# Hybrid encoder layer on one core: ten pairs of projection tiles by seven products each, attention two heads at a time beside a two-part output projection

## The chip, the cores and the metric

The kernel runs on one core of a Trainium2 chip. The time is device microseconds of one execution, from three runs. Everything is computed in float32; a float32 product is made exact from three products of shortened operands (below).

## The reference

768 tokens (512 of a prompt, 256 of a sample) of width 2048 pass one layer. What is computed, shortened:

```
h = rms_norm(x)                      # scale by (mean of x*x + eps) ** -0.5, times a gain per feature
p = h @ w_in                         # 2048 -> 8192 features, and 32 more for decay and beta
A: 8 heads x 128: softmax(q k^T / sqrt(128) + ALiBi and window bias) v, times SiLU(gate_A)
B: 8 heads x 128: short conv on q, k, v, gated delta rule in both directions,
   RMSNorm per head, times SiLU(gate_B)
y = rms_norm(x + concat(A, B) @ w_out)
```

## The kernel before

Features lie on the 128 partitions and tokens on the free axis, so the input projection makes 64 feature tiles of 128 x 768 tokens: tiles 0 to 7 q, 8 to 15 k, 16 to 23 v and 24 to 31 gate of the attention heads, 32 to 55 q, k and v and 56 to 63 gate of the delta heads. A tile runs over 16 K tiles of 128. Weights and inputs are split exactly into a high and a low part (`hip` and `lop` of the weights, `xh` and `xl` of the inputs), and `kstep` adds three products per K tile, high x high, high x low and low x high, each as one matmul of 512 columns (prompt, bank `mm_0`) and one of 256 (sample, bank `mm_1`): 96 matmuls of 384 columns in the mean for a tile, 6144 for all. The weights come as blocks of 128x512 (256 KB) and are split in pieces of 256 columns: ScalarE copies the high part, VectorE or, for every other piece, GpSimd subtracts it for the low part (`w_split`).

x is split as it arrives, before its norm is known: x times the gain is `xh_x`, `xl_x`, and the factor of each token (`rB`, the same in all partitions) is multiplied in after the products, by VectorE on the way out of PSUM (`normed` and `conv_post`). The sum of squares behind `rB` is added up in `x_squares`, mostly on GpSimd (`xacc`).

The order of the tiles stands in `jobs`: first the delta heads, q, k, v and the gate of the head before, then the attention heads one by one, q, k, v and a gate, with four attention gates after the last head, and at the end the output projection. While a tile is projected, `Driver` sets steps of other work between the groups of matmuls (`slot`): convolutions, the delta rule of one head, or one attention head (`attend`, tag `attend`, one at a time). `Driver` keeps a rough clock of each engine and takes, of the steps whose inputs are due, the one with the best priority; all this is settled when the program is built. Each engine then runs its own instructions in the order in which they were written, so an instruction that waits holds up all that stand behind it on the same engine.

In an attention head, S is scores (three products per tile of 128 queries), `s` the softmax on VectorE and ScalarE, T its transposes, PT the transposed weights split in two (ScalarE copies, VectorE subtracts), and o the product with v.

The output projection takes the 16 K tiles of the mixed features, delta heads first, in four quarters of 512 output columns and six tiles of 128 tokens: 48 matmuls of 128x512 for each group (`mmo`), 1152 in all, with nothing but the splitting of its own weights (`oh`, `ol`) and the end of each group (`o_post`: add the residual, square, gain) beside it. Three quarters go out to `yD` and come back for the last.

Instructions are recorded by helpers, so in the profile all matmuls have line L272, transposes L277, other operations L192 and loads or stores L234; in the changed kernel these are L280, L285, L200 and L242. Tiles are told apart by name.

Of the kernel before, what the change touches and what calls it, by code (L numbers as in the profile page):

```python
# [6 lines left out]
F32 = mybir.dt.float32  # L7
# [16 lines left out]
# columns of the constant array  # L24
# [3 lines left out]
def constants():  # L28
# [4 lines left out]
        # sums over the tokens up to i (from i on), counted from the middle of the tile  # L33
# [14 lines left out]
HOP = 0.12       # us from an instruction's end to one on another engine that waits for it  # L48
EARLY = 1.0      # us by which steps without products are emitted ahead of their inputs
SIDE_MAX = 3     # side steps between two groups of products  # L50
DEEP = 2.5       # us of work queued on VectorE beyond which bulk steps hold back
LOOK, AHEAD = 3, 4     # half stages by which weights are split, loaded ahead
DEC_P = 5        # priority of the decays
SUB_P, SUB_N, SUB_E = -6, 2, 1.0    # the inversions: priority, columns at a time, head start
LATE = 4         # attention gates that are projected after the last head


class Driver:
    """Orders the work as it is emitted. It keeps a rough clock of every engine; the projections' products run on,
    and the steps of the side tasks go between them once their inputs are due."""  # L60
# [32 lines left out]
    def ran(self, eng, cost, outs, ins, extra=0.0):  # L93
        """an instruction was emitted: its time by the rough clocks"""
# [10 lines left out]
    def placed(self, tag, ap, bufs):  # L105
        """a new tile in one of a tag's places: it waits for the place's last reader"""
# [16 lines left out]
    def free(self, tag, n=1):  # L123
        """can n more of the tag's places be had? (a place is given back once its last reader is emitted)"""
# [11 lines left out]
    def until(self, cond):  # L136
        """emit side steps until the condition holds"""
# [1270 lines left out]
```

## Time and profile before

| | |
|---|---|
| runs | 1663.59, 1667.91 and 1667.31 us, median 1667.31 |
| profiled execution | span 1662.0 us from its first to its last instruction, 1.6 us under the shortest run and 5.3 under the median; what lies around the span isn't shown apart |
| instructions | 27562, of them 10283 matmuls (transposes among them) |
| TensorE busy | 1615.9 us (97%) |
| VectorE busy | 841.0 us (51%) |
| ScalarE busy | 736.3 us (44%) |
| GpSimd busy | 416.3 us (25%) |
| traffic with memory | 125.65 MB read, 22.86 MB written, 89 GB/s over the span |

Busy time counts running instructions only. Matmuls overlap, so the mean duration of one (some 0.4 us for 512 columns) is longer than the distance between the starts of two; where a text speaks of the pace of matmuls it means that distance. In rows, PE is TensorE, DVE VectorE, ACT ScalarE, POOL GpSimd and SP the queue of loads and stores. "Idle before, releaser" and the waits name what ended an engine's idle time.

### The profile page before, as it was taken

The numbers are of one execution on the slowest core, as the hardware profiler recorded it, in microseconds if no ns is written. First come the engines' busy times: TensorE is split into PE (matmuls) and PEld (weight loads), VectorE is DVE, ScalarE is ACT, GpSimd is POOL, SyncE is SP. The second block draws the span as 40 slices with busy tenths as digits, with TensorE's granted clock in tenths as the row PEclk, the third lists the DMA queues.
The fourth block names the chain that finished last, engine by engine and source line by source line (L and its number), as shares of the span: only waits on it lengthen the run. The fifth ranks groups of instructions, "written<-read, shape, count | busy, mean of one in ns | idle before, by whom it ended". The sixth has DMA issues, their size and how long they took to land.

```text
span 1662.0 us, 27562 instructions
## 1 busy us (share of the span) xinstructions
PE 1615.9 (97%) x10283; PEld 1392.2 (84%) x10283; DVE 841.0 (51%) x1956; ACT 736.3 (44%) x1861; POOL 416.3 (25%) x430
## 2 busy tenths in 40 slices
PE   5999999999999999999999999999999999999997
PEld 4788788888888888898888888888888888888885
DVE  6758674857677767675343342425334336313132
ACT  5575546564765566553433232424333335202121
POOL 4443413232424242332121222222121210111100
PEclk9999999999999999999999999999999999999999
DMA  5232312232323232313212222221221256534365
GB/s 190 61 89 72 97 47 79 64 87 59 83 62 87 65 80 65 87 47 84 67 49 79 65 61 69 61 75 55 78 75 57 72 188 224 158 91 118 90 200 180
DMA packets 107783, 150.32 MB, mean 90 GB/s; under 512 B 40864, under 2 KB 48128, under 8 KB 107648
## 3 DMA queue, kind: packets, MB, share of 16 engines
q1 hardware_dynamic: 105632, 143.83, 29.8%
q10 hardware_dynamic: 2016, 4.72, 0.7%
q8 instruction: 81, 1.33, 0.3%
q14 instruction: 54, 0.44, 0.1%
HBM read 125.65 MB, written 22.86 MB: 89 GB/s over the span
## 4 chain that ended last, share of the span: by engine, by line
PE 78%; DVE 9%; DMA 5%; ACT 4%; issue 3%; SPq 1%; POOL 0%; DVEq 0%; POOLq 0%; ACTq 0%
PE mm L272 55%; PE mmo L272 11%; PE c L272 5%; DVE lop L192 2%; PE o L272 2%; PE S L272 2%; DMA res<-in_x 1%; PE m L272 1%; DVE tmp L192 1%; PE kk L272 1%; PE T L277 1%; DMA xst<-in_xT 1%; DVE cacc L192 1%; DMA st<-in_wt 1%; DVE PB L192 1%
## 5 line engine op out<-in xcount | busy, mean ns | idle before, releaser
L272 PE MATMUL mm<-xl_x,hip 128*128 128x512 f32 (+1 forms) x2048 | 541.4, 345 | 7.6 <-DVE xl_x L192 7.6
L272 PE MATMUL mm<-xh_x,hip 128*128 128x512 f32 (+1 forms) x2048 | 538.0, 344 | 8.8 <-ACT hip L192 7.7
L272 PE MATMUL mm<-xh_x,lop 128*128 128x512 f32 (+1 forms) x2048 | 539.5, 345 | 0.0
L192 POOL TENSOR_TENSOR lop<-st,hip 128x256 fp32r<-128x256 f32 x252 | 205.8, 817 | 817.7 <-ACT hip L192 744.9
L272 PEld LDWEIGHTS mm<-xh_x,hip 128*128 128x128 f32 x2048 | 315.1, 189 | 52.2 <-ACT hip L192 8.1
L272 PEld LDWEIGHTS mm<-xl_x,hip 128*128 128x128 f32 x2048 | 315.9, 190 | 49.3 <-DVE xl_x L192 9.2
L272 PEld LDWEIGHTS mm<-xh_x,lop 128*128 128x128 f32 x2048 | 316.6, 190 | 41.4
L192 ACT CAST hip<-st 128x256 fp32r<-128x256 f32 x512 | 202.0, 402 | 328.0 <-PE mm L272 254.3
L192 DVE TENSOR_TENSOR lop<-st,hip 128x256 fp32r<-128x256 f32 x260 | 146.9, 566 | 323.7 <-ACT hip L192 313.4
L272 PE MATMUL mmo<-oh,xh_m 128*128 128x512 f32 x384 | 151.7, 395 | 0.4 <-DVE yt_a L192 0.4
L272 PE MATMUL mmo<-ol,xh_m 128*128 128x512 f32 x384 | 151.7, 395 | 0.0
L272 PE MATMUL mmo<-oh,xl_m 128*128 128x512 f32 x384 | 151.6, 395 | 0.0
L192 DVE TENSOR_TENSOR PB<-PB,tmp 88x30 f32<-88x30 f32 (+14 forms) x240 | 91.4, 381 | 8.2
L192 DVE TENSOR_TENSOR tmp<-PB 88x30 f32<-88x30 f32 (+14 forms) x240 | 92.2, 384 | 6.1 <-ACT PB L192 1.5
L272 PEld LDWEIGHTS mmo<-oh,xh_m 128*128 128x128 f32 x384 | 72.4, 189 | 17.6 <-DVE yt_a L192 0.9
L272 PEld LDWEIGHTS mmo<-ol,xh_m 128*128 128x128 f32 x384 | 72.4, 189 | 16.8
L272 PEld LDWEIGHTS mmo<-oh,xl_m 128*128 128x128 f32 x384 | 72.5, 189 | 16.7
L192 DVE TENSOR_TENSOR yt<-mmo,res 128x512 f32<-128x512 f32 x18 | 12.4, 690 | 126.9 <-PE mmo L272 92.6
L192 POOL TENSOR_TENSOR cacc<-cacc,ctmp 128x772 f32<-128x772 f32 x32 | 58.9, 1841 | 58.3 <-ACT ctmp L192 54.2
L192 ACT ACTIVATE s<-s,m 128x512 f32<-128x512 f32 (+1 forms) x48 | 31.3, 653 | 92.8 <-DVE m L192 92.8
L192 POOL TENSOR_TENSOR yt<-yt,fg 128x512 f32<-128x512 f32 x18 | 23.2, 1291 | 190.5 <-ACT res L192 190.5
L192 ACT ACTIVATE res<-yt 128x512 f32<-128x512 f32 x18 | 11.4, 632 | 132.7 <-DVE yt L192 132.7
(198 smaller groups left out, 1880.7 us busy)
## 6 DMA issues: line engine op xcount, KB each, us to landing
st<-in_wt SPq DMA_DIRECT2D x256, 256.0 KB
ost<-in_wo SPq DMA_DIRECT2D x32, 512.0 KB
dec<-gcD SPq DMA_DIRECT2D x24, 256.0 KB
xl_m<-mixD SPq DMA_DIRECT2D x16, 384.0 KB
res<-in_x SPq DMA_DIRECT2D x24, 256.0 KB
out_y<-row SPq DMA_DIRECT2D x12, 512.0 KB
xst<-in_xT SPq DMA_DIRECT2D x15, 384.0 KB
yD<-yt SPq DMA_DIRECT2D x18, 256.0 KB
```

Source lines behind the costliest of these rows:

```text
L192: r = f(*a, **k)
L272: r = PE.matmul(out, lhsT, rhs, start=start, stop=stop)
L277: r = PE.transpose(out, in_, ident)
```

## The change

**Input projection.** Ten pairs of feature tiles (v of all attention heads, their gates, and four delta gates) are computed by Strassen's scheme in Winograd's form. For a pair, rows are two feature tiles, columns the two halves of 384 tokens, and K goes in two phases of 2 x 4 K tiles; in each phase seven products of 4 K tiles take the place of eight (`PRODUCTS`, `pair_products`), every one with three matmuls of 384 columns per K tile: 84 a phase, 168 a pair, where two tiles had 192. The combinations of the weights (S1 to S4) are made by VectorE as the weights come, those of the inputs (T1 to T4) once for all pairs (`block_sums`), and the products are combined out of three PSUM banks X, Y and Z by VectorE (`evacuate`). Weights are split 512 wide, in a ring of six tiles.

**Order.** Four delta gates are projected first, two tiles at a time on x as it arrives. Then x is normalised in place (`norm`, new `xh_n` and `xl_n`), q and k of the first attention head follow tile by tile behind it, then the ten pairs, then the other 38 tiles singly. The multiplications with `rB` behind the projections fall away but for those four gates. q, k, v and gates of the attention heads wait in memory (`qD`, `kD`, `vD`, `agD`, `gD`) till they are needed. The additions of squares go from GpSimd to VectorE.

**Attention and output projection.** Two heads run at a time on two sets of buffers (`SETS`), from the time that the 24 convolutions are done, on into the output projection. This has two parts: part 0 the eight K tiles of the delta heads, for all 24 groups, with the attention beside it; part 1 the eight of the attention heads, to which part 0's result comes back from `yD`. The products with v are taken for two query tiles at a time, 256 columns wide.

```diff
+ORDER, FIRST_ORDER = (1, 6, 5, 2, 7, 3, 4), (1, 2, 5, 6, 3, 7, 4)
+PRODUCTS = {1: ("A11", "X", "B11"), 2: ("A12", "X", "B21"), 3: ("S4", "Z", "B22"), 4: ("A22", "Y", "T4"),
+            5: ("S1", "Z", "T1"), 6: ("S2", "Y", "T2"), 7: ("S3", "Y", "T3")}
...
-                        (V if k >= NK - 2 else G).tensor_tensor(out=xacc, in0=xacc, in1=s, op=ALU.add)
+                        V.tensor_tensor(out=xacc, in0=xacc, in1=t, op=ALU.add)
...
+            def plan_pair(pi, ph, order):
+                f0, f1 = pairs[pi]
+                c0, c1 = 2 * ph, 2 * ph + 1
+                names = dict(A11=(f0, c0), A21=(f1, c0), A22=(f1, c1), A12=(f0, c1))
...
+                            V.tensor_tensor(out=s["S1"], in0=a("A21"), in1=a("A22"), op=ALU.add)
+                            V.tensor_tensor(out=s["S2"], in0=s["S1"], in1=a("A11"), op=ALU.subtract)
+                            V.tensor_tensor(out=a("A21"), in0=a("A11"), in1=a("A21"), op=ALU.subtract)
+                            s["S3"] = a("A21")
...
+                        if name == "S4":
+                            s["S4"] = a("A12")
+                            V.tensor_tensor(out=s["S4"], in0=s["S4"], in1=s["S2"], op=ALU.subtract)
+                        src = s[name] if name in s else a(name)
+                        r = w_split(src, f"p{m}")
...
+            def inputs(ph, name, i):
+                lo, hi = slice(0, HALF), slice(HALF, T)
+                a, b = 8 * ph + i, 8 * ph + 4 + i
+                if name in ("B11", "B21", "B22", "T2"):
+                    k, c = {"B11": (a, lo), "B21": (b, lo), "B22": (b, hi), "T2": (a, hi)}[name]
+                    return xh[k][:, c], xl[k][:, c]
+                t = tset[ph, name, i]
+                return t[:, lo], t[:, hi]
...
+                for n, pr in enumerate(order):
+                    _, b, name = PRODUCTS[pr]
+                    drv.until(lambda: there(ph, name))
+                    new = b not in x["banks"]
+                    if new:
+                        drv.until(lambda: free("mm"))
+                        take("mm")
+                        x["banks"][b] = bank(f"{b}{pi}_{ph}")
+                    else:
+                        drv.until(lambda: all(q in x["ev"] for q in order[:n] if PRODUCTS[q][1] == b))
+                    u, (hi, lo) = piece()
+                    for i in range(4):
+                        v = inputs(ph, name, i)
+                        c = slice(i * P, i * P + P)
+                        for m, (w, j) in enumerate(((hi, 0), (hi, 1), (lo, 0))):
+                            mm(x["banks"][b][:, :HALF], w[:, c], v[j], start=(new and i == 0 and m == 0), stop=(i == 3 and m == 2),
+                               more=True)
+                            if i < 3 or m < 2:
+                                drv.slot()
+                    done_with(u)
+                    drv.end = drv.t + HOP
+                    spawn(evacuate(x, pr), -20)
...
+                need = {1: (), 2: (1,), 3: (5, 6), 4: (5, 6, 7), 5: (1,), 6: (1,), 7: (5, 6)}[pr]
...
+                if pr == 1:
+                    A.copy(s1, X[:, :HALF])
+                elif pr == 6:
+                    V.tensor_tensor(out=u2, in0=Y[:, :HALF], in1=s1, op=ALU.add)
+                    add(u2, 1)
+                elif pr == 5:
+                    V.tensor_tensor(out=t5, in0=Z_[:, :HALF], in1=s1, op=ALU.add)
+                    add(t5, 3)
+                else:
+                    q = {2: 0, 3: 1, 7: 3, 4: 2}[pr]
...
+                    if pr == 2 and not ph:
+                        A.copy(d, X[:, :HALF])
+                    else:
+                        V.tensor_tensor(out=d, in0={2: X, 3: Z_, 7: Y, 4: Y}[pr][:, :HALF], in1={2: d, 3: u2, 7: t5, 4: s1}[pr],
+                                        op=ALU.add)
...
+            def norm():
+                for k in range(NK + 1):
+                    if k < NK:
+                        yield from wait(lambda: reached["raw"] > k)
+                        xn = xstage[k]
+                        V.scalar_tensor_tensor(out=xn, in0=xn, scalar=g_in[:, k:k + 1], in1=rB, op0=ALU.mult, op1=ALU.mult)
+                        xtiles(k, "n")
+                        A.copy(xh[k], xn)
+                    if k:
+                        p = k - 1
+                        V.tensor_tensor(out=xl[p], in0=xstage[p], in1=xh[p].bitcast(F32), op=ALU.subtract)
+                        normal.add(p)
...
+                yield from diff("T1", xa[:, hi], xa[:, lo])
+                yield from high("T1")
+                yield from diff("T2", xb[:, hi], t["T1"])
+                yield from high("T2")
+                low("T1")
+                yield AHEAD
+                yield from diff("T4", xb[:, lo], t["T2"])
+                low("T2")
+                yield from diff("T3", xb[:, hi], xa[:, hi])
+                give(f"t{a}", f"t{a + 4}")
+                yield from high("T4")
+                yield from high("T3")
+                low("T4")
+                low("T3")
+                yield AHEAD
...
-                        V.tensor_tensor(out=cin[:, o:o + width[h]], in0=ps[h][:, :width[h]], in1=rB[:, parts[h]], op=ALU.mult)
+                        A.copy(Z["cin"][:, o:o + width[h]], ps[h][:, :width[h]])
...
+            SETS = (dict(vT="cin", V=("vtok", "vtok"), tab="XT", g="cacc"), dict(vT="ctmp", V=("oacc", "DN"), tab="PB", g="PBT"))
...
+            pairs = ([(16 + j, 17 + j) for j in range(0, NH, 2)] + [(24 + j, 25 + j) for j in range(0, NH, 2)]
+                     + [(56 + j, 57 + j) for j in (4, 6)])
...
+            chain_o = [(part, n, j) for part in (0, 1) for n in range(NQ) for j in range(NH)]
...
+                        ps = bank(f"o{part}{n}_{t}")
+                        o_fetch(part, n, t)
+                        for j in range(NH):
+                            ostep(ps, part, t, j)
+                            between(j)
+                            if t == NT - 1 and j and (part, n) != (1, NQ - 1):
+                                o_split()
+                            drv.slot()
```

On VectorE, the turn from the first to the second phase of the second pair (`lop69` is the low part of the first weights of phase 1, `out1_1` a quarter of the pair's result, mmY and mmZ the banks):

```order
L200 TENSOR_TENSOR lop67_1834<-st35_1716,hip67_1833 128x512
L200 TENSOR_TENSOR sum2_92<-mmZ1_0_1812,sum0_90 128x384
L200 TENSOR_TENSOR lop68_1851<-st34_1676,hip68_1850 128x512
L200 TENSOR_TENSOR lop69_1873<-st36_1718,hip69_1872 128x512
L200 TENSOR_TENSOR out1_1_1877<-mmY1_0_1793,sum2_92 128x384
L200 TENSOR_TENSOR S1_1_1_1890<-st37_1759,st38_1817 128x512
L200 TENSOR_TENSOR S2_1_1_1891<-S1_1_1_1890,st36_1718 128x512
L200 TENSOR_TENSOR st37_1759<-st36_1718,st37_1759 128x512
L200 TENSOR_TENSOR lop70_1896<-S2_1_1_1891,hip70_1895 128x512
```

Nothing of this stood in the kernel before, where VectorE had one subtraction per piece of weights. Product 4 writes bank Y after product 7 has been taken out of it by `out1_1`, which stands behind `lop69`.

On VectorE, the end of the normalisation and the first of eight blocks of input combinations (`xl_n` the low part of normalised x, T1 to T4 the combinations, f as they are and s split; `raw` weights of the gates 58 and 59):

```order
L200 SCALAR_TENSOR_TENSOR xst15_155<-xst15_155,g_in_93,rB_98 128x768
L200 TENSOR_TENSOR xl_n14_1187<-xst14_153,xh_n14_1186 128x768
L200 TENSOR_TENSOR raw43_1205<-st21_999,raw43_1205 128x256
L200 TENSOR_TENSOR raw44_1210<-st22_1031,raw44_1210 128x256
L200 TENSOR_TENSOR xl_n15_1196<-xst15_155,xh_n15_1195 128x768
L200 TENSOR_TENSOR T1f0_1228<-xst0_112 128x384
L200 TENSOR_TENSOR T2f0_1232<-xst4_127,T1f0_1228 128x384
L200 TENSOR_TENSOR T1s0_1230<-T1f0_1228,T1s0_1230 128x384
L200 TENSOR_TENSOR T4f0_1246<-xst4_127,T2f0_1232 128x384
L200 TENSOR_TENSOR xl_n0_714<-T2f0_1232,xh_n0_713 128x384
L200 TENSOR_TENSOR T3f0_1249<-xst4_127,xst0_112 128x384
L200 TENSOR_TENSOR T4s0_1251<-T4f0_1246,T4s0_1251 128x384
```

These are new too: 16 times the two of the normalisation, eight times eight of the combinations.

On TensorE, one attention head before, between matmuls of a projected tile (S4_2: scores of head 4, query tile 2; T4_0_0: transposes of its tile 0):

```order
L277 MATMUL T4_0_0_12559<-ident_404,s4_0_12487 128x128 x4
L272 MATMUL mm5_0_12397<-xh_x13_376,hip414_12472 128x512
L272 MATMUL mm5_1_12398<-xh_x13_376,hip414_12472 128x256
L272 MATMUL mm5_0_12397<-xl_x13_377,hip414_12472 128x512
L272 MATMUL mm5_1_12398<-xl_x13_377,hip414_12472 128x256
L272 MATMUL mm5_0_12397<-xh_x13_376,lop414_12474 128x512
L272 MATMUL mm5_1_12398<-xh_x13_376,lop414_12474 128x256
L272 MATMUL mm5_0_12397<-xh_x14_396,hip415_12502 128x512
L272 MATMUL mm5_1_12398<-xh_x14_396,hip415_12502 128x256
L272 MATMUL mm5_0_12397<-xl_x14_397,hip415_12502 128x512
L272 MATMUL mm5_1_12398<-xl_x14_397,hip415_12502 128x256
L272 MATMUL S4_2_12582<-khi4_12125,qhi4_11899 128x512
```

and in the change, between groups of part 0 of the output projection, heads 2 and 3:

```order
L285 MATMUL T2_4_0_13924<-ident_157,s2_4_13808 128x128 x2
L280 MATMUL S3_2_13929<-khi3_13648,qhi3_13636 128x512
L280 MATMUL S3_2_13929<-qklo3_13567,qhi3_13636 128x512
L280 MATMUL S3_2_13929<-khi3_13648,qklo3_13567 128x512
L280 MATMUL mmo0_2_13706<-oh6_13901,xh_m6_13574 128x512
L280 MATMUL mmo0_2_13706<-ol6_13902,xh_m6_13574 128x512
L280 MATMUL mmo0_2_13706<-oh6_13901,xl_m6_13575 128x512
L285 MATMUL T2_4_1_13947<-ident_157,s2_5_13911 128x128 x2
L280 MATMUL mmo0_0_13704<-oh7_13941,xh_m7_13583 128x512
L280 MATMUL mmo0_0_13704<-ol7_13942,xh_m7_13583 128x512
L280 MATMUL mmo0_0_13704<-oh7_13941,xl_m7_13584 128x512
L280 MATMUL o2_4_1_13958<-PT2_13474,V02_13363 128x256 x4
```

Steps of attention that had ten and more matmuls of a projection between them now stand three output matmuls apart, and belong to two heads.

## Rows read from the trace of the kernel before

**Rows 1.** The page: span, busy time of each engine, chain that ended last.
```profile
span 1662.0 us, 27562 instructions
PE 1615.9 (97%) x10283; PEld 1392.2 (84%) x10283; DVE 841.0 (51%) x1956; ACT 736.3 (44%) x1861; POOL 416.3 (25%) x430
PE 78%; DVE 9%; DMA 5%; ACT 4%; issue 3%; SPq 1%; POOL 0%; DVEq 0%; POOLq 0%; ACTq 0%
```

**Rows 2.** Windows: length, busy us (instructions) by engine, TensorE's granted clock, DMA.
```profile
0.00:40.00 40.00, 23.36 (x102) 17.52 (x102) 26.68 (x24) 21.80 (x33) 19.27 (x13) 0.96 0.58 197
40.00:80.00 40.00, 37.42 (x203) 30.64 (x204) 32.35 (x51) 18.77 (x34) 18.78 (x20) 0.96 0.22 62
...
520.00:560.00 40.00, 36.93 (x368) 31.55 (x367) 22.73 (x56) 27.86 (x73) 17.12 (x18) 1.00 0.35 89
...
1400.00:1440.00 40.00, 40.00 (x174) 32.46 (x173) 5.77 (x9) 4.29 (x11) 5.12 (x4) 1.00 0.39 119
```

**Rows 3.** Waits of TensorE over the span: us in total, times, longest.
```profile
PE mm L272 <- ACT hip L192: 7.7, 2, 7.3
PE kk L272 <- DVE in L192: 7.7, 3, 4.0
PE mm L272 <- DVE xl_x L192: 7.6, 5, 3.1
PE ab L272 <- DVE hab L192: 4.2, 1, 4.2
```

**Rows 4.** The chain in order of time: start, length, what; a stretch of matmuls alone.
```profile
1011.88 36.76 PE mm L272 x212
```

**Rows 5.** Timeline of TensorE: start, duration, instruction; matmuls of 256 columns.
```profile
1156.07 0.28 PE L272 MATMUL S<-khi,qhi 128*128 128x256 f32 x1
...
1156.31 0.28 PE L272 MATMUL S<-khi,qklo 128*128 128x256 f32 x1
```

**Rows 6.** Windows of the start, columns as in rows 2.
```profile
20.00:56.00 36.00, 28.37 (x138) 21.52 (x137) 32.85 (x22) 16.74 (x25) 27.80 (x19) 0.91 0.40 134
32.00:34.00 2.00, 2.00 (x7) 1.45 (x7) 2.00 (x3) 0.35 (x1) 1.50 (x1) 0.50 0.28 70
```

**Rows 7.** Timeline of the start, VectorE and GpSimd.
```profile
9.87 1.02 DVE L192 SCALAR_TENSOR_TENSOR xl_x<-xst,g_in,xh_x 128x768 fp32r<-128x768 f32 x1 [1.65 <-ACT xh_x L192]
...
21.84 6.93 POOL L192 TENSOR_TENSOR xacc<-xacc,xst 128x768 f32<-128x768 f32 x3
...
24.49 2.58 DVE L192 SCALAR_TENSOR_TENSOR xl_x<-xst,g_in,xh_x 128x768 fp32r<-128x768 f32 x1
```

**Rows 8.** Groups of instructions by shape: busy us, mean ns, idle before.
```profile
L192 DVE TENSOR_TENSOR ol<-ost,oh 128x512 fp32r<-128x512 f32 x64 | 42.6, 716 | 17.4 <-ACT oh L192 17.2
...
L192 DVE TENSOR_TENSOR PTl<-T,PTh 128x384 fp32r<-128x384 f32 x32 | 17.7, 554 | 10.5 <-ACT PTh L192 10.5
...
L192 DVE TENSOR_TENSOR xl_m<-xl_m,xh_m 128x768 fp32r<-128x768 f32 x16 | 14.9, 974 | 3.1 <-ACT xh_m L192 3.0
```

**Rows 9.** Groups of ScalarE: the high part of the output weights.
```profile
L192 ACT CAST oh<-ost 128x512 fp32r<-128x512 f32 x64 | 36.2, 617 | 18.4 <-DMA ost<-in_wo 13.5 <-DVE yt_a L192 2.4 <-PE mmo L272 2.2
```

**Rows 10.** Timeline of one attention head.
```profile
1135.15 0.39 PE L272 MATMUL S<-khi,qklo 128*128 128x512 f32 x1
...
1137.50 0.60 PE L277 MATMUL T<-ident,s 128*128 128x128 f32 x4
1137.55 0.49 DVE L192 TENSOR_SCALAR s<-s,m 128x512 f32<-128x512 f32 x1
...
1138.65 0.56 DVE L192 TENSOR_TENSOR PTl<-T,PTh 128x384 fp32r<-128x384 f32 x1 [0.62 <-ACT PTh L192]
...
1139.84 0.43 DVE L192 TENSOR_TENSOR lop<-st,hip 128x256 fp32r<-128x256 f32 x1
```

**Rows 11.** Timeline of the end.
```profile
1650.76 0.39 PE L272 MATMUL mmo<-oh,xl_m 128*128 128x512 f32 x1
1652.50 0.69 DVE L192 TENSOR_TENSOR row<-mmo,res 128x512 f32<-128x512 f32 x1 [6.55 <-DMA res<-in_x]
```

More of the change, by code (lines that the diff above doesn't have):

```diff
@@ new lines, in quarter, with over, prepare @@
+            def quarter(f, c):
+                return wt[f][:, c * 512:(c + 1) * 512]
+            def over(n):
+                dead.add(n)
+                stages.pop(n)
+            def prepare(upto):
+                while cur["made"] <= min(upto, len(plan) - 1):
+                    m = cur["made"]
+                    size, last, make = plan[m]
+                    feed()
+                    if last >= cur["load"] or live and cur["w"] + size - 6 > min(live.values()):
+                        assert m > cur["used"]
+                        break
+                    live[m] = cur["w"]
+                    made[m] = make(m)
+                    cur["w"] += size
+                    cur["made"] += 1
+                feed()
@@ new lines, in attend, with product @@
+                give(S["vT"])
+                yield from get("intra")
+                both = st("intra", (2, 4, 256), f"PT{h}", F32R)
+                qT, kT = (qkv.pop((h, w)) for w in "qk")
+                qkv.pop((h, "lo"))
+                def product(ps, ls, rs):
+                    for c, (l, r) in enumerate(((0, 0), (0, 1), (1, 0))):
+                        m = len(rs[0])
+                        for i in range(m):
+                            mm(ps, ls[l][i], rs[r][i], start=(c == 0 and i == 0), stop=(c == 2 and i == m - 1))
@@ L1082, in attend @@
+                yield lambda: drv.ready(tab) and drv.ready(g)
+                prev = None
+                for t0, t1 in tiles6:
+                    for qi in range(t1 - t0):
+                        s = yield from scores(t0, t1, qi)
                         if prev is not None:
@@ new lines, in leave, with ostep @@
+            def leave(k):
+                left.add(k)
+            for n, (f, post) in enumerate(single):
+                last = n == len(single) - 1
+                if last:
+                    spawn(m_first(), -3)
+                    spawn(w_first(), -2)
+                project(f, post, leave if last else None)
+            def ostep(ps, part, t, j):
+                hi, lo = wset[j]
+                ts = slice(t * P, (t + 1) * P)
+                m = mset[part][j]
+                mm(ps, m[0][:, ts], hi, start=(j == 0), stop=False)
+                mm(ps, m[0][:, ts], lo, start=False, stop=False)
+                mm(ps, m[1][:, ts], hi, start=False, stop=(j == NH - 1))
@@ L1307, in o_post @@
-                if n < NQ - 1:
+                A.activation(ps, yt, AF.Square, accum_out=late["sums"][:, t, n:n + 1])
+                (V if row else G).tensor_tensor(out=yt, in0=yt, in1=gains[n], op=ALU.mult)
+                if not row:
                     return
-                r = op.tile([P, 2], F32, tag="r", name=f"r{t}", bufs=2)
-                V.tensor_reduce(out=r[:, 0:1], in_=sums[:, t], axis=AX.X, op=ALU.add)
+                r = small([2], "r", f"r{t}")
+                V.tensor_reduce(out=r[:, 0:1], in_=late["sums"][:, t], axis=AX.X, op=ALU.add)
@@ L1371, in layout @@
+            while pend or done:
+                between(1)
+                between(3)
+            op_cm.__exit__(None, None, None)
 def layout(i):
```

956 lines of the change are left out of this document (555 added, 401 removed).

## The prediction

> **What bounds the kernel now.** I read the page first, then windows of 40 us, the waits of TensorE, and single stretches. The reader is to see that TensorE is the bound nearly everywhere: it is busy for 1615.9 of 1662.0 us, and the chain that ended last is TensorE for 78% [rows 1]. The other 46.1 us are not spread evenly. By 80 us it has stood idle for 16.6 + 2.6 = 19.2 us [rows 2], made up of three waits: 7.3 for the first weights, 7.6 for low parts of x from VectorE, 4.2 for the split of the small weights [rows 3]. After the last matmul (1650.76) come 11 us of output [rows 11]. The remaining 16 us lie mostly among the delta heads, as in 520 to 560 us, where 3.1 us are lost [rows 2], half of it in waits for one product's input on VectorE, 7.7 us in three [rows 3]. In the output projection nothing is lost: 174 matmuls of 512 columns in 40.00 us, 0.230 us each [rows 2]. So removed matmuls count in full, and new work on VectorE counts where TensorE has to wait for it.
>
> **1. Fewer matmuls.** Twenty tiles need 20 x 84 = 1680 matmuls of 384 columns in place of 1920 of 512 and 256. In the stream of projections 212 matmuls, 384 columns in the mean, take 36.76 us, 0.1734 each [rows 4]. 240 x 0.1734 = **-41.6**. No matmul of 384 columns stands in the trace; 512 columns scaled give 0.230 x 0.75 = 0.1725 [rows 2], 256 columns, 0.24 us for two, give 0.12 x 1.5 = 0.18 [rows 5]. If the 1680 cost that instead of 0.1734 the term runs from -43 to -30; I take the mean that the stream shows, since both widths are in it. The Trainium skill, "TensorE: Matmul & The Clock Gate", section Back-to-back issue gap, has N/2.4 + 2.5 ns for a lone matmul, 162.5 ns at 384 columns; 240 of those would be -39.0, an estimate from that page. The row decides, as the page itself restricts its formula, and 512 columns here take 230 ns against its 216.
>
> **2. The start.** The additions of squares leave GpSimd, where three ran from 21.84 to 28.77 us; beside them a split of x on VectorE took 2.58 us, alone 1.02 [rows 7]. Over 20 to 56 us VectorE was busy for 32.85 of 36 us and TensorE idle for 7.6 [rows 6]. Now VectorE adds them itself: 15 more operations of 768 at about 0.97 [rows 8], 15 us, against 16 x 1.5 us saved on the splits, and it is less full. Two tiles are projected on each arriving K tile, so TensorE has twice as much to do per arrival. I take away the 7.6 of low parts and 1.7 of the 4.2 for the small weights, and add 1.6 for the matmul of the norm, which now sits inside the stream: -7.7, taken as **-7**. Bounds: 0, if VectorE is as late as now, and -12, both waits gone.
>
> **3. VectorE until the first pair is done.** This is the price in front. From the norm on VectorE must do 16 x (1.02 + 0.97) = 31.8 us of normalisation [rows 7, 8], 64 combinations of 384 at 0.554 = 35.5 [rows 8], 32 pieces of weights of 256 at 0.43 = 13.8 [rows 10], and the first pair, 22 operations of 512 at 0.7 plus 13 of 384 at 0.554 = 22.6; with some 2 for the gating's small operations, 106 us. TensorE has for this 4 tiles of 96 x 0.1734 = 66.6 and one pair of 168 x 0.1734 = 29.1, 96 us. The difference stays: **+10**. Low end 0, if the pair can start on its first combinations while the last are made; high end 30, if ScalarE's copy stands between each two of a chain of combinations.
>
> **4. Waits inside a pair.** In the steady state VectorE needs 22.6 us of the 29.1 of a pair, so throughput holds. But product 4 needs bank Y, which product 7 leaves only through `out1_1`, and this stands on VectorE behind the next phase's first `lop`. That `lop` needs a place in the ring, free at the end of product 7. From there: ScalarE's copy of 512 0.617 [rows 9], `lop` 0.716, `out1_1` 0.554 [rows 8], and some 0.4 for three hand-overs make 2.3 us; product 3 between covers 12 x 0.1734 = 2.1. Product 4 waits 0.2, in second phases, where sums stand in front as well, up to 0.9. 20 phases x 0.4 = **+8**, bounds 0 and 18.
>
> **5. Delta heads.** Multiplications with the norm leave VectorE for copies on ScalarE, and GpSimd splits half as many weights. Of the 13 us lost there I give back **-4**; bounds -13 and, as ScalarE takes the copies over, +5.
>
> **6. Attention beside the output projection.** The steps of two heads now stand about three output matmuls apart. From the end of S (about 1135.5) to normalised weights (1138.04) passed 2.5 us, from the start of T (1137.50) to the low part of its split (1139.21) 1.7 [rows 10]. With another head's work between, some 9 us of TensorE's work lie from S to T and 2.1 from T to o, so nothing waits as long as VectorE isn't behind. It is at three turns of quarters, where the splits of new weights, following their predecessor's last products, hold up softmax: **+4**, bounds 0 and 20. Products with v in two halves of 256 cost the same per column [rows 5].
>
> **7. Turn to the second part.** Mixed features of the last heads go out and come back, covered by three groups of 24 x 0.230 = 5.5 us each [rows 2]: **+2**, bounds 0 and 12, where the last store lands late.
>
> **8. Tail.** The last addition waited 1.3 us for its loaded operand [rows 11]; it is now asked for a whole group earlier: **-1**.
>
> Sum: -41.6 - 7 + 10 + 8 - 4 + 4 + 2 - 1 = -29.6. From the span of 1662.0 this gives 1632.4; the median lies 5.3 above the profiled span, so the forecast is **1638**. A change within 0.3% (5 us) can't be told from none.
>
> **The rivals.** *A, the new waits don't come.* Terms 3 and 4 go to 0, since VectorE may work ahead by the buffers there are: -47.6, 1620. For it speaks that VectorE is busy for only 51% [rows 1]; against it, that terms 3 and 4 are chains, not averages. Chance 0.20.
>
> *B, the gain is eaten.* Terms 3 and 4 at their upper ends, 30 and 18: +0.4, 1668. For it speak rows 7, where VectorE was late by 2.5 times its lone duration; against it, that GpSimd, which did that, has nothing in this stretch. Chance 0.07.
>
> *C, the clock.* After the waits of the start TensorE ran at a granted 0.50, its 1.2 GHz, from 32 to 34 us, and 0.91 in the mean over 36 us [rows 6]. If the waits of terms 3 and 4 do the same over the 96 us in front of the first pair, 9% of it, 9 us, are added: 1647. The rule behind it is in the Trainium skill, "TensorE: Matmul & The Clock Gate", Part 1: pauses throttle the array, activity releases it. By that rule the pauses of the wall would cost twice; the trace agrees only for the start. Chance 0.13.
>
> *D, slower: VectorE becomes the bound through all ten pairs.* The point from which it decides: two tiles took 2 x 96 x 0.1734 = 33.3 us, and VectorE's 22.6 us per pair reach that at 1.47 times their lone durations. At 1.8 times a pair takes 40.7, 10 x (40.7 - 29.1) = +116 in place of term 4, together 1738. For it speaks the factor 2.5 in rows 7; against it, that no GpSimd work stands beside the pairs. The Trainium skill, "SBUF — State Buffer", section Who interferes with whom, names an exclusive port between VectorE with two inputs in SBUF and a reading GpSimd; rows 7 agree, and by it this rival fails. Chance 0.06.
>
> **How the numbers follow.** The forecast itself, 1626 to 1650 by one or two terms off, has 0.54. Faster by over 0.3% (under 1662) are it, A, C and a little of B: 0.87. Same are most of B: 0.05; slower D and the rest of B: 0.08. The range leaves out D, most of B, and A where other terms fall low as well: 1608 to 1662.
>
> **What would show it.** In the profile after: 10139 matmuls (240 fewer, 96 more from halves); pairs of 29 to 30 us each; waits of TensorE for `out1` of 0.2 to 0.9 us in pairs, 20 of them; VectorE without a pause from the norm to the first pair, TensorE waiting there for `xl_n` or T1 to T4; a split of x of 1.0 us at the start. The prediction is wrong if a matmul of 384 columns shows another pace than 0.173, if TensorE's first 150 us lose less than 12 us in all or over 45, or if attention costs the output projection more than 20 us.

## The result: slower by 3%, and the profile after

The change takes 1715.16 us (median of four runs, 1714.38 to 1716.2) against 1666.16 us of the kernel before on the same chip: a ratio of 1.0297, 95% interval 1.0283 to 1.0312. The forecast was 1638, and faster. The profiled execution of the change has a span of 1712.7 us, where the forecast had 1632.4.

The page of the change, to be held against [rows 1]:

```profile
span 1712.7 us, 27316 instructions
PE 1605.5 (94%) x10139; PEld 1409.9 (82%) x10139; DVE 1045.0 (61%) x2199; ACT 790.7 (46%) x1784; POOL 259.4 (15%) x225
...
PE 59%; DVE 15%; DMA 9%; ACT 7%; issue 6%; POOL 3%; SPq 2%; DVEq 0%; ACTq 0%; POOLq 0%
```

The 10139 matmuls are the count forecast. But TensorE's share of the chain went from 78% to 59%, and two sums are off. Its idle time is 1712.7 - 1605.5 = 107.2 us; before it was 46.1 [rows 1]. And its busy time should be 1615.9 - 41.6 = 1574.3 us; it is 31 us more.

TensorE's waits of the change (us in total, times, longest), to be held against [rows 3]:

```profile
PE tro L285 <- DVE gate L200: 18.1, 3, 6.0
PE m L280 <- DMA DN<-DD: 17.8, 14, 3.8
PE mmr L280 <- ACT xh_x L200: 10.3, 1, 10.3
PE mmX L280 <- ACT sum L200: 9.1, 1, 9.1
PE trv L285 <- ACT vT L200: 8.7, 4, 6.3
PE mm L280 <- POOL lop L200: 6.8, 6, 1.8
PE mmo L280 <- ACT oh L200: 4.1, 4, 1.6
PE mmo L280 <- DVE ol L200: 3.1, 8, 1.1
PE mmZ L280 <- DVE sum L200: 3.0, 1, 3.0
PE mmY L280 <- DVE out L200: 1.8, 2, 1.2
```

The two largest and the fifth are new, and belong to the delta heads: tro (transposes of a head's output), m (products of the inversion, whose blocks DN come by a detour through memory) and trv (transposes of v). From 440 to 1340 us, the stretch of the delta heads, all waits add up to 55.2 us; in the kernel before, from 60 to 820, to 12.8.

Windows of the change, columns as in [rows 2]; the stretch with the wall (the waits in the first pair), a stretch of pairs, one delta head, the end:

```profile
120.00:160.00 40.00, 27.62 (x134) 25.12 (x133) 36.85 (x73) 20.96 (x43) 0.00 (x0) 0.81 0.19 63
...
200.00:240.00 40.00, 40.00 (x231) 39.60 (x230) 29.79 (x52) 12.94 (x22) 0.00 (x0) 1.00 0.31 93
...
920.00:960.00 40.00, 33.97 (x332) 28.95 (x331) 20.44 (x45) 11.79 (x24) 6.06 (x6) 0.91 0.32 93
...
1680.00:1720.00 40.00, 15.90 (x69) 12.55 (x67) 9.43 (x20) 7.50 (x12) 2.17 (x4) 0.83 0.65 230
```

The pairs are without a gap: 231 matmuls in 40 us, 0.173 each. The head at 920 us loses 6 us to one wait, and its mean clock is 0.91. Where that comes from is seen in three short windows behind the wait:

```profile
921.00:927.00 6.00, 0.32 (x2) 0.00 (x0) 5.54 (x15) 0.31 (x1) 0.00 (x0) 0.93 0.37 136
927.00:929.00 2.00, 1.64 (x6) 1.45 (x7) 1.90 (x6) 0.00 (x0) 0.00 (x0) 0.50 0.00 0
929.00:931.00 2.00, 2.00 (x9) 1.81 (x8) 1.90 (x7) 0.00 (x0) 0.00 (x0) 0.50 0.07 25
```

After 6 us without work TensorE runs at 0.50, 1.2 GHz, and is busy all the time with little more than half the work: two matmuls of 512 and 256 columns start every 0.64 us there (at 928.5), every 0.35 before the wait (at 912). That is the second sum: busy time grows with the waits. The Trainium skill, "TensorE: Matmul & The Clock Gate", Part 1, has the two levels and a throttle that activity releases; the trace agrees.

What kept VectorE, in the timeline of the same head (start, duration, instruction):

```profile
912.00 1.86 POOL L200 TENSOR_TENSOR cacc<-cacc,ctmp 128x772 f32<-128x772 f32 x1 [5.18 <-ACT ctmp L200]
912.14 1.99 DVE L200 TENSOR_TENSOR PB<-PB,tmp 88x238 f32<-88x238 f32 x1
...
913.81 1.44 POOL L200 TENSOR_TENSOR lop<-st,hip 128x512 fp32r<-128x512 f32 x1
...
914.16 1.35 DVE L200 TENSOR_TENSOR tmp<-PB 88x240 f32<-88x240 f32 x1
...
916.28 2.00 POOL L200 TENSOR_TENSOR cacc<-cacc,ctmp 128x772 f32<-128x772 f32 x1
...
916.60 1.95 DVE L200 TENSOR_TENSOR PB<-PB,tmp 88x240 f32<-88x240 f32 x1
...
922.74 0.39 DVE L200 TENSOR_TENSOR tmp<-PB 88x220 f32<-88x220 f32 x1
...
926.56 0.74 DVE L200 SCALAR_TENSOR_TENSOR gate<-tro,dng,gate 128x512 f32<-128x512 f32 x1
...
927.36 0.69 PE L285 MATMUL tro<-ident,oa 128*128 128x128 f32 x2 [6.03 <-DVE gate L200]
```

An operation on PB or tmp of this width takes 0.4 us, but 1.4 to 2.0 where an addition (`cacc`) or a split (`lop`) of GpSimd runs. An inversion is a chain of 60 operations on PB and tmp. The three shown and one of 1.14 us at 919.41 lose 4.8 us together; VectorE has fallen behind, and `gate`, for which TensorE waits 6.03 us, stands in its queue behind them. During the wait itself VectorE runs at full pace. The groups say the same. In the kernel before (mean ns of one after the comma):

```profile
L192 DVE TENSOR_TENSOR lop<-st,hip 128x256 fp32r<-128x256 f32 x260 | 146.9, 566 | 323.7 <-ACT hip L192 313.4 <-PE mm L272 6.9 <-PE tro L277 2.5
...
L192 DVE TENSOR_TENSOR PB<-PB,tmp 88x30 f32<-88x30 f32 (+14 forms) x240 | 91.4, 381 | 8.2
L192 DVE TENSOR_TENSOR tmp<-PB 88x30 f32<-88x30 f32 (+14 forms) x240 | 92.2, 384 | 6.1 <-ACT PB L192 1.5
```

and in the change:

```profile
L200 DVE TENSOR_TENSOR lop<-st,hip 128x512 fp32r<-128x512 f32 x176 | 124.8, 709 | 177.1 <-ACT hip L200 175.2 <-DMA st<-in_wt 1.6
L200 DVE TENSOR_TENSOR PB<-PB,tmp 88x30 f32<-88x30 f32 (+14 forms) x240 | 114.7, 478 | 8.2
...
L200 DVE TENSOR_TENSOR tmp<-PB 88x30 f32<-88x30 f32 (+14 forms) x240 | 102.0, 425 | 22.3 <-ACT PB L200 15.8
```

PB and tmp together take 217 us in place of 184. VectorE's own splits, on the other hand, are hardly stretched any more: 0.709 against 0.69 where GpSimd does none of this work (run e8_conv, below), where those of 256 took 0.566 against 0.43 [rows 10].

Is GpSimd busier beside the delta heads than before? Its two large jobs there, in the kernel before from 60 to 820 us:

```profile
L192 POOL TENSOR_TENSOR lop<-st,hip 128x256 fp32r<-128x256 f32 x137 | 113.1, 827 | 395.2 <-ACT hip L192 331.5 <-PE mm L272 48.2 <-PE c L272 7.4
L192 POOL TENSOR_TENSOR cacc<-cacc,ctmp 128x772 f32<-128x772 f32 x32 | 58.9, 1841 | 58.3 <-ACT ctmp L192 54.2 <-PE mm L272 3.4
```

and in the change from 440 to 1340 us:

```profile
L200 POOL TENSOR_TENSOR lop<-st,hip 128x512 fp32r<-128x512 f32 x75 | 105.3, 1405 | 854.2 <-ACT hip L200 815.8 <-DVE s L200 14.3 <-PE mm L280 11.4
L200 POOL TENSOR_TENSOR cacc<-cacc,ctmp 128x772 f32<-128x772 f32 x32 | 60.5, 1892 | 51.9 <-ACT ctmp L200 51.9
```

It is not: 172 us before, 166 in the change. What differs is what they fall on. Each operation on PB and tmp was held against the same shape in run e8_conv, where neither job runs on GpSimd. By the timelines those that are longer by over 0.1 us lose 58 us in the change, 34 of it beside additions and 22 beside splits; in the kernel before they lose 27, 5 of it beside additions and 19 beside splits.

### The profile page after: what moved, and what is told of

It is laid out like the page before. It is cut to its first block, busy times and chain, and to the rows that moved or that the text cites. A ratio compares the mean times of both kernels' runs of the same rounds, so it can differ in the third digit from the quotient of the medians.

```text
span 1712.7 us, 27316 instructions
## 1 busy us (share of the span) xinstructions
PE 1605.5 (94%) x10139; PEld 1409.9 (82%) x10139; DVE 1045.0 (61%) x2199; ACT 790.7 (46%) x1784; POOL 259.4 (15%) x225
## 4 chain that ended last, share of the span: by engine, by line
PE 59%; DVE 15%; DMA 9%; ACT 7%; issue 6%; POOL 3%; SPq 2%; DVEq 0%; ACTq 0%; POOLq 0%
PE mm L280 21%; PE mmo L280 10%; PE mmY L280 7%; PE mmX L280 5%; PE mmZ L280 4%; PE c L280 4%; DVE tmp L200 4%; DVE PB L200 3%; DMA out_y<-row 2%; SPq L242 2%; PE o L280 1%; PE S L280 1%; PE m L280 1%; PE kk L280 1%; DVE cacc L200 1%
## 5 line engine op out<-in xcount | busy, mean ns | idle before, releaser
L280 PE MATMUL mm<-xh_n,lop 128*128 128x512 f32 x1216 | 326.6, 350 | 8.1 <-POOL lop L200 6.8
L280 PE MATMUL mm<-xl_n,hip 128*128 128x512 f32 x1216 | 327.0, 350 | 0.0
L280 PE MATMUL mm<-xh_n,hip 128*128 128x512 f32 x1216 | 324.5, 348 | 1.2 <-ACT hip L200 1.2
L200 ACT CAST hip<-st 128x512 fp32r<-128x512 f32 x252 | 154.1, 617 | 229.1 <-PE mm L280 88.4
L200 POOL TENSOR_TENSOR lop<-st,hip 128x512 fp32r<-128x512 f32 x76 | 106.6, 1404 | 867.8 <-ACT hip L200 829.5
L200 DVE TENSOR_TENSOR lop<-st,hip 128x512 fp32r<-128x512 f32 x176 | 124.8, 709 | 177.1 <-ACT hip L200 175.2
L280 PEld LDWEIGHTS mm<-xh_n,lop 128*128 128x128 f32 x1216 | 189.5, 192 | 35.1 <-POOL lop L200 9.2
L280 PEld LDWEIGHTS mm<-xh_n,hip 128*128 128x128 f32 x1216 | 189.4, 192 | 26.0 <-ACT hip L200 1.8
L280 PEld LDWEIGHTS mm<-xl_n,hip 128*128 128x128 f32 x1216 | 189.8, 192 | 24.6
L200 DVE SCALAR_TENSOR_TENSOR cacc<-cin,cw,cacc 128x772 f32<-128x772 f32 x64 | 74.6, 1165 | 13.2 <-ACT cacc L200 11.7
L280 PE MATMUL mmo<-ol,mh 128*128 128x512 f32 x192 | 76.2, 397 | 1.7 <-DVE ol L200 1.7
L280 PE MATMUL mmr<-xh_x,raw 128*128 128x512 f32 (+1 forms) x256 | 60.6, 349 | 10.3 <-ACT xh_x L200 10.3
L200 POOL TENSOR_TENSOR res<-res,fg 128x512 f32<-128x512 f32 x18 | 23.2, 1295 | 301.9 <-DMA res<-yD 235.3
```

The costliest lines, as they stand in the source:

```text
L200: r = f(*a, **k)
L280: r = PE.matmul(out, lhsT, rhs, start=start, stop=stop, skip_group_check=more)
```

## The experiments

**Which cause: GpSimd beside VectorE, or an order drawn too tight?** The change also raised by 7% the cost of a matmul with which the planner (`Driver`) reckons, to what a matmul really takes. So fewer matmuls stand in front of every step that TensorE waits for. Two edits, apart and together.

```diff
-                    plan.append((2, len(loads) - 1, make(len(loads) - 1, G if c % 2 else V)))
+                    plan.append((2, len(loads) - 1, make(len(loads) - 1, V)))
```

> In the 38 single tiles all weights are split on VectorE, none on GpSimd. Theory A (GpSimd's subtractions of 128x512, 1.4 us each, hold up VectorE, whose chain of 30 small operations per inversion then ends 4 to 6 us after its place in the order): the operations on PB and tmp, 217 us in the change, fall to 175 or less, TensorE's waits for tro, DN, trv and lop among the delta heads fall from 53 us to 20 or less, the clock stays at 1.00 there, and the time falls from 1715 to about 1665. Theory B (the order is drawn up with a truer pace of matmuls and has lost the slack that the kernel before had): the waits stay above 40 us, and with 76 x 0.7 = 53 us more on VectorE the time is 1705 to 1730.

Measured: 1651.53 us, 0.9908 of before (0.9893 to 0.9923). PB and tmp 173.6 us, the waits among the delta heads 12.7 us, busy time of TensorE 1585.0. These are the marks of theory A, and the time is 13 below the one named. But the planner draws a new order, too: GpSimd's additions, which are untouched, cost PB and tmp 15 us here in place of 34. Run e11_read below keeps the order.

```diff
-            c = 1.07 * max(n, 256)
+            c = max(n, 256)
```

> The planner's matmul costs what it did in the kernel before (n columns in place of 1.07 n), so that every chain on VectorE is given 7% more matmuls to hide behind; nothing else is changed. Theory B (lost slack): waits among the delta heads fall from 53 us to 25 or less with PB and tmp still at 200 us or more; time about 1670. Theory A (contention): a chain of 25 us gains less than 2 us of slack, too little for waits of 4 to 6; the waits stay above 35 us and the time above 1695.

Measured: 1689.63 us, 1.0129 (1.0106 to 1.0153); waits 23 us with PB and tmp at 196. That is more than theory A allowed, and the time is 20 above the one of theory B. With more room in the order, part of VectorE's delay is hidden or doesn't arise (PB and tmp lose 21 us less, with the same work on GpSimd): 26 us of 64. It costs in another place: one wait of 14.6 us at the turn to the second part of the output projection.

> Both edits, splits on VectorE and the old pace. Theory A: no better than the splits on VectorE alone, within 6 us. Theory B: no better than the old pace alone. If both causes add, 10 to 25 us below the better of the two, 1645 to 1655.

Measured: 1668.98 us, 1.0021 (1.0009 to 1.0033), worse than the first edit alone by 17, which none of the three cases named. Its waits among the delta heads are few (9.0 us), but in the output projection TensorE waits 10.3 us at the turn and 11.8 for `oh`, against none and 2.9 with the first edit alone. So the truer pace is right as soon as VectorE keeps to it; the old one helps against the delay only.

**Are the seven products to blame?**

```diff
-                    pair_products(pi, ph, ORDER if pi or ph else FIRST_ORDER, kinds[pi], pair_hook(pi))
+                for f, (kind, h) in zip(pairs[pi], kinds[pi]):
+                    project(f, spill_post(kind, h))
```

> The ten pairs are projected as 20 single tiles at the same place, without block sums or products by sevens; all else is the change. If the products give what was reckoned (240 matmuls, 41.6 us) and cost a wall of 12 us and a slow clock of some 7 behind it, this is 20 to 25 us slower than the change, 1735 to 1740. If Strassen's products are what made the change slow, it is faster than the change, 1700 or less.

Measured: 1743.96 us, 1.046 (1.0428 to 1.0493), 28.8 slower than the change, a little more than was named, with the same waits among the delta heads (tro 18.1, DN 18.6). So the products are not to blame: of the 41.6 us that they save they cost 13, by difference.

**What of GpSimd's work: its length, its sum, its place?** First the same subtractions in two halves:

```diff
-            E.tensor_tensor(out=lo, in0=src, in1=hi.bitcast(F32), op=ALU.subtract)
+            for c in (slice(0, 256), slice(256, 512)) if E is G else (slice(0, 512),):
+                E.tensor_tensor(out=lo[:, c], in0=src[:, c], in1=hi[:, c].bitcast(F32), op=ALU.subtract)
```

> The change itself, with each of GpSimd's subtractions of 512 columns cut into two of 256, as wide as in the kernel before; where they stand is the same. If the length of one subtraction is what hurts (VectorE blocked for the whole of it), PB and tmp fall from 217 us to 190 or less and the time to 1690 or less. If it is the sum of GpSimd's work that hurts, which is the same, both stay within 10: PB and tmp above 207, time 1705 to 1725.

Measured: 1710.08 us, 1.0271 (1.0256 to 1.0287), PB and tmp 215.0: not the length. Then VectorE and GpSimd each on half of the same weights at the same time, in all quarters of a tile:

```diff
+            for F, c in ((V, slice(0, 256)), (G, slice(256, 512))) if E is G else ((V, slice(0, 512)),):
+                F.tensor_tensor(out=lo[:, c], in0=src[:, c], in1=hi[:, c].bitcast(F32), op=ALU.subtract)
```

> The change, with GpSimd's share of the splits the same in columns (half of every tile), but cut so that VectorE subtracts columns 0 to 255 and GpSimd 256 to 511 of the same weights at the same time, as the kernel before had it. If VectorE's delay by GpSimd does harm only where it falls on the inversions, and the kernel before let it fall on splits (its lop 0.57 us in the mean against 0.43 alone): lop of 256 on VectorE goes to 0.55 or more, PB and tmp fall from 217 to 195 or less, the time to 1695 or less. If only the sum of GpSimd's work counts, PB and tmp stay above 207 and the time at 1705 to 1720.

Measured: 1698.81 us, 1.0193 (1.0175 to 1.0211). The groups of this run:

```profile
L200 DVE TENSOR_TENSOR lop<-st,hip 128x256 fp32r<-128x256 f32 x152 | 85.8, 566 | 180.1 <-ACT hip L200 166.9 <-DMA XT<-DX 6.4 <-DMA st<-in_wt 3.0
...
L200 DVE TENSOR_TENSOR tmp<-PB 88x30 f32<-88x30 f32 (+14 forms) x240 | 109.2, 455 | 7.9 <-ACT PB L200 2.3
L200 DVE TENSOR_TENSOR PB<-PB,tmp 88x30 f32<-88x30 f32 (+14 forms) x240 | 94.4, 393 | 8.2
```

The splits of 256 are back at the 566 ns of the kernel before, and PB and tmp at 203.6 are better by 13 us, not by the 22 that were named. The time stands 3.8 above the bound named, 16 below the change, and 43 us of waits are left among the delta heads. The time did fall while VectorE's delay moved to the splits, but how much that did isn't shown: beside splits PB and tmp lose 20 us in place of 22, and most of what they gained stands beside the additions, 25 in place of 34, which only the new order moved.

**Is it the reading of SBUF?** The next edit takes GpSimd's other large work away too, the additions in the convolutions of v:

```diff
-                        if ctile >= 16:
+                        if ctile >= 24:
```

> The splits on VectorE as before, and the convolutions of the delta heads' v, whose additions (32 of 1.9 us) were GpSimd's, as four operations on VectorE like those of q and k. If GpSimd's remaining work still stretches the inversions, PB and tmp fall from 174 us to about 160, the remaining waits of some 14 us among the delta heads to half, and the time by 5 us or more; if what is left there is VectorE's own load (34 us more of it now), the time rises by up to 10.

Measured: 1634.87 us, 0.9817 (0.9801 to 0.9834). PB and tmp 157.0 us, the waits among the delta heads 3.3:

```profile
L200 DVE TENSOR_TENSOR PB<-PB,tmp 88x30 f32<-88x30 f32 (+14 forms) x240 | 78.8, 328 | 8.3
L200 DVE TENSOR_TENSOR tmp<-PB 88x30 f32<-88x30 f32 (+14 forms) x240 | 78.2, 326 | 5.6 <-ACT PB L200 0.4
```

On this kernel idle work was laid on GpSimd, 75 times, in one run as subtractions, in another as fills; its results are not used, and the order of all else stays:

```diff
+                        if E is G and junk:
+                            nc.gpsimd.tensor_tensor(out=junk[0], in0=r[0][:, :448].bitcast(F32), in1=junk[0], op=ALU.subtract)
```

> The change with both moves to VectorE, and beside it 76 idle subtractions on GpSimd (448 columns, two inputs in SBUF, about 1.2 us each, started where its splits stood; nobody uses the result). The order of all else is that of the kernel without them (1634.9). If it is the reading of SBUF by GpSimd that holds VectorE up: PB and tmp from 157 to 180 or more, time 1655 to 1690. If the change was slow because results came late from GpSimd, or by the order: PB and tmp within 5 of 157, time within 5 of 1635.

Measured: 1661.36 us, 0.9974 (0.9961 to 0.9988), 26 us more than without. VectorE's groups, and what ran on GpSimd:

```profile
L200 DVE TENSOR_TENSOR PB<-PB,tmp 88x30 f32<-88x30 f32 (+14 forms) x240 | 91.6, 382 | 8.3
L200 DVE TENSOR_TENSOR tmp<-PB 88x30 f32<-88x30 f32 (+14 forms) x240 | 91.5, 381 | 5.2
...
L534 POOL TENSOR_TENSOR junk<-hip,junk 128x448 f32<-128x448 f32 x75 | 108.3, 1443 | 561.1 <-ACT hip L200 561.1
```

```diff
+                        if E is G and junk:
+                            nc.gpsimd.tensor_tensor(out=junk[0][:, :8], in0=r[0][:, :8].bitcast(F32), in1=junk[0][:, :8], op=ALU.subtract)
+                            nc.gpsimd.memset(junk[0], 0.0)
+                            nc.gpsimd.memset(junk[0], 0.0)
+                            nc.gpsimd.memset(junk[0], 0.0)
```

> The same, with the idle work as three fills of 448 columns (1.2 us together, no input but 8 columns to start them). If only GpSimd's reads hold VectorE up: PB and tmp within 5 of 157, time within 5 of 1635. If any work of GpSimd does: as the run with the subtractions.

Measured: 1646.94 us, 0.988 (0.9861 to 0.9899), 12 us more.

```profile
L200 DVE TENSOR_TENSOR PB<-PB,tmp 88x30 f32<-88x30 f32 (+14 forms) x240 | 78.8, 328 | 8.3
L200 DVE TENSOR_TENSOR tmp<-PB 88x30 f32<-88x30 f32 (+14 forms) x240 | 78.3, 326 | 5.5 <-ACT PB L200 0.4
```

With subtractions PB and tmp take 183 us, 26.1 of the 26.3 us more in operations that run beside a subtraction; with fills they take 157.1, as without idle work. So it is GpSimd's reading of SBUF that holds VectorE, whoever uses the result. The Trainium skill, "SBUF — State Buffer", section Who interferes with whom, says that VectorE with two inputs in SBUF contends with a GpSimd instruction that reads SBUF, not with one that only writes; both runs agree.

The 12 us of the fills, 7 above the bound named, must have another cause, as PB and tmp show none. The idle work stands in GpSimd's own queue ahead of the decays and norms of the delta heads, and it reads `hip`: ScalarE waits 23.2 us for decays in place of 12.4, and 17.8 for the idle work itself. That this makes the 12 us is argued, not shown, and part of the 26 may be the same. So the reading costs some 14 to 26 us here, by the two runs, of the 80 that lie between the change and this kernel. The rest comes with the same two jobs, but no run parts it into the reading of the additions, later results of GpSimd and the new order.

**Does the kernel before gain by the same edits?** All its splits and the convolutions of v on VectorE:

```diff
-                    pieces[p] = w_split(stages[p // 2], c, f"p{p}", G if p % 2 and p > 7 else V)
+                    pieces[p] = w_split(stages[p // 2], c, f"p{p}", V)
```

> The kernel before, with the same two things taken from GpSimd: all weights are split on VectorE, and the convolutions of v and the splits of attention's q and k run there too. If GpSimd's work costs wherever it stands beside the inversions, the kernel before gains as well: its 13 us of waits among the delta heads halve, 1655 to 1662. If the kernel before hid it (its order left room, and its contended operations were splits that nobody waited for), it stays at 1666 within 4 us or gets slower by VectorE's added load.

Measured: 1684.47 us, 1.0108 (1.0091 to 1.0125), slower by 19. PB and tmp fall to 156.8 there too, but the waits among the delta heads rise to 18.5 us, for steps of ScalarE (`z`) and VectorE, and TensorE's busy time grows by 15.0 us, at a granted 0.98 in place of 1.00 from 60 to 820 us. Only 12.8 us of waits stood there to be gained, and the relief on PB didn't gain them.

**Two heads at a time** (on the kernel with splits on VectorE):

```diff
-            sets, turn = [0, 1], [0]
+            sets, turn = [0], [0]
```

> The splits on VectorE as before, and one attention head at a time. If two at a time are what lets the attention hide beside part 0, one at a time runs past its end, and the time grows by 15 us or more over 1651.5. If one head's chain is short enough, within 5 us.

Measured: 1736.61 us, 1.0431 (1.0413 to 1.045), 85 more. Its waits from 1270 to 1620 us:

```profile
PE T L285 <- DVE s L200: 18.4, 12, 2.7
PE o L280 <- ACT PT L200: 12.4, 11, 1.6
PE mmo L280 <- ACT mh L200: 10.5, 1, 10.5
```

One head's chain isn't covered: attention runs past part 0 and stands alone, with the granted clock at 0.67 from 1500 to 1600 us.

**The tail** (splits on VectorE):

```diff
-                set_pool(op, dict(row=(4 * KB, 4), fg=(2 * KB, 2)))
+                set_pool(op, dict(row=(4 * KB, 8), fg=(2 * KB, 2)))
```

> The splits on VectorE as before, and eight places in place of four for the rows of the last quarter, so that the queue isn't held by loads into rows still being stored. If the tail (16 us from the last matmul, against 11 in the kernel before) is late because of these places, it falls to 11 and the time to about 1646; if it is set by the bytes that the last quarter has to move in half the time, it stays within 2 us of 1651.5.

Measured: 1648.63 us, 0.9898 (0.9878 to 0.9918), 2.9 less. In the change the last matmul started at 1695.50 and the span ended at 1712.7, 17 us later; here it is 1635.12 and 1646.3, 11 us:

```profile
1635.12 0.40 PE L280 MATMUL mmo<-oh,ml 128*128 128x512 f32 x1
...
1637.38 0.69 DVE L200 TENSOR_TENSOR row<-mmo,res 128x512 f32<-128x512 f32 x1 [1.27 <-DMA res<-yD]
```

In the change the queue of loads and stores waited for rows still being stored, from 1640 us on:

```profile
SPq L242 <- DMA out_y<-row: 19.2, 8, 5.3
```

Here that wait is gone. The places were the cause of the longer tail. What they are worth in time is less sure, since the ranges of the two runs touch. **The sum of what helped**, both moves to VectorE and the eight places:

> The change with both moves to VectorE and the eight places for rows: the two gains add, 1634.9 less 3 to 5, 1630 to 1632.

Measured: 1630.02 us, 0.9781 (0.9765 to 0.9797): 2.2% faster than the kernel before, 85 us below the change. The eight places are worth 4.9 us here, and the runs with and without them don't overlap.

**The wall** (on that kernel):

```diff
-                    V.tensor_tensor(out=d[n][1], in0=t[n], in1=d[n][0].bitcast(F32), op=ALU.subtract)
+                    G.tensor_tensor(out=d[n][1], in0=t[n], in1=d[n][0].bitcast(F32), op=ALU.subtract)
```

> The fastest kernel so far (1630.0), with 32 subtractions of 384 columns of the block sums moved from VectorE to GpSimd, in the wall in front of the first pair (9.1, 2.5 and 3.1 us of waits). If VectorE's load alone makes the wall, 32 x 0.47 = 15 us less takes it away: 1615 to 1622. If GpSimd beside VectorE gives back what it takes, as among the delta heads, the time is 1627 to 1640.

Measured: 1636.6 us, 0.9818 (0.9801 to 0.9836), 6.6 more. The longest wait of the wall grew from 9.1 to 11.5 us:

```profile
PE mmX L280 <- ACT sum L200: 12.2, 2, 11.5
...
PE mmY L280 <- ACT T3s L200: 3.5, 1, 3.5
```

VectorE's combinations T1f to T4f took 0.71 to 0.79 us beside GpSimd's, in place of 0.55, and GpSimd took 1.1 to 1.3 us for a subtraction that VectorE does in 0.55. So the move costs more than it gives here, too. Whether less work for VectorE, with none for GpSimd, would remove the wall stays untried.

## Why the prediction was wrong

By its own terms, each against what the change's trace shows:

- **Term 1, held.** 0.173 us for a matmul of 384 columns, 240 fewer: -41.6. The estimate by the Trainium skill, "TensorE: Matmul & The Clock Gate", section Back-to-back issue gap, -39.0, was the worse one.
- **Term 2, held, in part by luck.** TensorE was idle for 10.3 + 1.4 = 11.7 us by 80 us, against 19.2: -7.5, forecast -7. The waits for low parts are gone and a split of x takes 1.0 us, as said. But the small weights cost nothing any more, where 2.5 were left to them, and the first matmul waits 3.0 us longer, which was not foreseen.
- **Term 3, held.** Waits of 9.1 and 3.0 us, both in the first pair, forecast +10. The longer one is not for `xl_n` or T1 to T4, as named: it is for ScalarE's copy of product 1 out of its bank (`sum`), which stands in ScalarE's queue behind copies of the combinations that VectorE is late with. Rival C added to it there: 134 matmuls took 27.6 us between 120 and 160, 4 more than at 0.173 each.
- **Term 4, oversized.** 1.8 us in two waits, in the first two pairs, forecast +8; none in the other eight. The chain behind `lop` is as described, but in the steady state nothing waits at the turn.
- **Term 5, the step that failed.** "I give back -4": it counted what leaves VectorE and how many instructions GpSimd loses, and concluded less delay. The waits went from 12.8 to 55.2 us, +42, far beyond the bounds (-13 and +5). What it left out is on which instructions GpSimd's remaining work falls: 166 us of splits and additions in place of 172, and yet 58 us lost on PB and tmp in place of 27. It also put the planner's new matmul cost at nothing, on which 26 us hang (run e2_pace). [Rows 7] had the effect, 2.58 us for 1.02; the prediction used it for the start, and in rival D only to ask whether GpSimd stood beside the pairs. It never asked what stood beside GpSimd in the stage where its work remained.
- **Terms 6 and 7, about right.** 6.9 us of waits from the start of the output projection to 1570 us, forecast +4 and +2.
- **Term 8, wrong sign.** 17 us in place of 11, +6, forecast -1; the operand is asked for earlier, but its load stands in a queue that waits for a row still being stored. In the last quarter a group lasts half as long as before.
- **Rival C, the clock: right mechanism, wrong place and size.** It was priced for the wall, 9 us. The busy time is 31 us above its count, most of it behind the waits of the delta heads: with these gone (3.3 us) it is 1575.7, and the count is 1574.3.

Together: 1662.0 - 41.6 - 7.5 + 14 (terms 3 and 4) + 42 + 7 (terms 6 and 7) + 6 + 31 = 1713, the span is 1712.7. The run without GpSimd's two large jobs comes to 1634.87, against the forecast of 1638. That bears out the other terms, but so near it is luck: there the waits in pairs are 5 below term 4 and those among the delta heads 5 below term 5, and the tail is 7 above term 8.

The mechanism of rival D was right for another stage: VectorE slowed by GpSimd, not through the pairs, where GpSimd does nothing, but among the delta heads. Its price has a slip: the forecast of 1638 with +116 in place of term 4 is 1746, not 1738.

What stays open: why the kernel before stood GpSimd's work so well. Nearly all of the difference on PB and tmp is the additions, which cost 5 us there and 34 in the change; the order is the likely reason, but no run takes the additions alone out of the change. Two traits of the kernel before were tried in the change, its lower matmul cost in the planner (26 us) and splits side by side (16 us), and each takes a part; that they add up to the whole isn't shown. Nor is it shown why the kernel before got slower by 19 us with that work gone; its order was then drawn anew, and other steps came late.

## What to carry to other kernels

Before counting an engine as free, look which instructions run beside it, and not only how busy it is: in the timeline a delayed operation of VectorE shows no idle time, only a longer duration, so compare each group's mean with that of the same shape where nothing runs beside it. Where steps are placed by a plan, a few us of delay on one engine become waits of the bound engine at every step queued behind, and each of these costs again by the slower clock after it. A move that halves the time per group also halves the time in which loads and stores of that group have to be done.

## What the runs showed of the hardware that was not expected

VectorE's operations on PB and tmp took up to 1.99 us for 0.4 beside GpSimd's reads, and with GpSimd filling, what they took without the fills (157.1 and 157.0 us for 480). Cutting GpSimd's reads in two left that delay as it was (215.0 and 216.7 us). And the price of a wait was nearly double its length: 42 us of new waits among the delta heads came with most of 31 us of busy time at 1.2 GHz.
